# Output projection weights of a hybrid decoder layer: second and third quadrant loaded after the fifth head pair's scores, their differences after the last pair's

## The chip, the cores and the metric

The kernel runs on one core of a Trainium2 chip. The metric is the device time of one execution in microseconds (us); the median of three runs before the change is 560.33 us (558.85 to 560.89). In the profile the engines are called PE (TensorE, matrix products), DVE (VectorE), ACT (ScalarE), POOL (GpSimd) and SP (SyncE, which only issues transfers). Each engine runs its instructions in the order in which the program lists them, so an instruction that waits holds up everything listed behind it on the same engine.

## The reference

One decoder layer on 512 positions of width 1024, in 32-bit floats:

```python
h = rmsnorm(x, norm1_w)
proj = h @ w_in                      # columns for three groups of heads
y_a = dilated_attention(...)         # 6 heads of 64
y_b = gla(...)                       # 4 heads, gated linear attention
y_c = moba_attention(...)            # 6 heads of 64; 512 positions: every past block is taken
mix = concatenate([y_a, y_b, y_c])   # 512 x 1024
x = x + mix @ w_out                  # output projection, w_out 1024 x 1024
h2 = rmsnorm(x, norm2_w)
x = x + square(relu(h2 @ w_ff1)) @ w_ff2
return rmsnorm(x, final_norm_w)
```

The change touches when the weights `w_out` are loaded and when sums of them are made.

## The kernel before

**Precision.** Every large product is made of three: weights and activations are each split into a high part (`wh`, `xh`, `Ah`: a copy by ACT to the reduced float type) and a low part (`wl`, `xl`, `Al`: a subtraction by DVE), and high x high, high x low and low x high are added up in one accumulator bank. `parts` (line 311) does this for a weight block of 128x1024 numbers; it is called by the one stream `cut` (line 333), which takes the blocks one after another, each when one of five pairs of split buffers is free.

**Stages in the order of time.** First a projection for the gated linear attention; then value products (`vps`, in `v_proj`), query and key products of six pairs of heads (`qkps`), the attention of the six pairs; then the second set of value products, the output projection (`ff2(0)`, tiles `f2X`, `f2W`, `f2Y`), and the feed-forward layer. The twelve attention heads are worked as pairs p = 0 to 5, so the "fifth pair" of the title is p = 4 and the last one p = 5.

**Attention of one pair** (`attention`, line 887, one stream for each of the two heads e). A table `nb` of position biases (128x512, 256 KB) is fetched by SP; the one for pair p + 1 is fetched in the middle of pair p. Scores are made on PE for four query blocks in the order 3, 2, 1, 0 into a bank of tag `s` (tile `sps`); there are two such banks. `softmax` (line 994) adds the bias and takes the minimum on DVE (`P<-sps,nb`, which frees the bank) and the exponential on ACT. When the scores of both heads of pair p are listed, the event `("scored", p)` is fired, and for the last pair also the event `"scores"`. The probabilities of pairs 0 to 4 are turned in `moved` (line 1019) and `back` (line 1044): DVE transposes 32x32 blocks (`tb`, `t2s`), SP writes them to DRAM (`turn`), and POOL reads them back in the other order (`thb`, `th`). After the store of both heads the event `("sent", p)` is fired. The last pair is turned by products on PE instead (`ptp`). `values` (line 949) then multiplies probabilities and values, two pairs at a time (tile `po`).

**Output projection.** The 1024x1024 matrix product is done as 2 x 2 quadrants with seven products instead of eight, so sums of quadrants are needed on both sides. The weights' quadrants are called (0,0), (1,1), (0,1), (1,0) in the order of their loading; each is two blocks of 512 KB (`woraw`). `fetch0` (line 444) lists the loads on SP. `sums0` (line 457) makes the sums on DVE:

```python
for ip in range(2):
    t[ip] = b22[ip] - b12[ip]      # product 4, second in order; b22 is (1,1), b12 is (0,1)
for ip in range(2):
    b12[ip] = b12[ip] - b11[ip]    # product 3
```

later `t + b11` for product 2, and `b21 - t` for product 6. `products` (line 494) gives the order of the seven: 0, 4, 6, 2, 3, 1, 5.

**The order of work.** The program is not listed by hand: some thirty streams (Python generators) each yield one operation at a time, and `Plan` (line 112) simulates them while the program is being built. It takes the operation that could start first by its own estimate (at a tie the lower priority number, then the older stream), adds it to its engine's list and moves that engine's clock on. A yield of ("wait", event) or ("take", resource) holds a stream back in this planning. Transfers are modelled as one line of 360 KB per us, longer by a factor for the turned data (line 149); then a time is added until the data count as arrived (line 150): `ZL` for the small transfers of the softmax sums (`zt`), `PL` for POOL's plain transfers, 0.9 us for the others. So any number in the model can change the order of the lists, though no operation is added or lost. On the chip semaphores keep the order correct whatever the estimates; where an estimate is wrong, an engine waits.

All operations are recorded by one helper, so every instruction of the profile has line 142 (L142); they are told apart by the tiles' names.

Of the kernel before, what the change touches and what calls it, by code (L numbers as in the profile page):

```python
# [27 lines left out]
LC, LT, LW, LN, WARM = 1.0, 0.5, 1.0, 0.0, 9  # L28
BIGS, SLOTS, WPAIRS, SCRATCH = 43, 22, 5, 2048
NC = 5  # L30
ZL, PL = 5.0, 3.4
LATE = ((1, 0),)
XP = (0, 1, 2, 3, 4)
NH = 4

# [76 lines left out]
class Plan:  # L112
# [15 lines left out]
    def spawn(self, gen, prio=0):  # L128
        self.streams.append(dict(gen=gen, prio=prio, item=None, at=self.now, sent=None, n=len(self.streams)))

    def fire(self, key, t=None):
        self.done[key] = self.now if t is None else t

    def give(self, res):
        self.free[res].append(self.now)
# [5 lines left out]
    def issue(self, op, at):  # L141
        getattr(getattr(self.nc, op.eng), op.method)(*op.args, **op.kw)  # L142
        t = self.start(op, at)
        if op.eng in self.part:
            self.part[op.eng] = op.part
        self.clock[op.eng] = end = t + op.cost
        if op.method == "dma_start":
            self.clock["dge"] = max(self.clock["dge"], t) + 0.47
            self.clock["dma"] = max(self.clock["dma"], self.clock["dge"] + 0.65) + op.size / 360e3 * (1 + 0.2 * ("turn" in op.outs[0] + op.ins[0]))
            end = self.clock["dma"] + (ZL if op.outs[0][:2] == "zt" else 0.9 if op.eng != "gpsimd" or "accum_op" in op.kw else PL)  # L150
        for n in op.outs:
            self.ready[n] = max(self.ready.get(n, 0.0), end + self.LAT)
        return end
# [57 lines left out]
def hybrid_block_kernel(ctx: ExitStack, tc: tile.TileContext, x0_d, xT_d, x_d, w0_d, wv_d, wqk_d, w1_d, w2_d,  # L211
# [16 lines left out]
    def big(name, dt=F32, shape=(128, 1024)):  # L228
        return wp.tile(list(shape), dt, name=name, tag="big", bufs=BIGS)
# [214 lines left out]
    def fetch0():  # L444
        yield ("wait", ("sent", 3))
        spawn(sums0(), 3)
        for q in ((0, 0), (1, 1), (0, 1), (1, 0)):
            quads[q] = []
            if q in LATE:
                yield ("wait", "vT")  # L450
            for ip in range(2):
                yield ("take", "big")
                quads[q].append(big("woraw"))
                yield SP.dma_start(quads[q][ip], w2_d[0, q[0], q[1], ip])
            fire(("quad", 0, q))

    def sums0():

        yield ("wait", ("quad", 0, (0, 0)))
        t, b6 = [None] * 2, [None] * 2  # L460
        b11 = quads[0, 0]
        B[0] = {0: b11, 4: t, 2: t, 6: b6}
        fire(("B", 0, 0))
        yield ("wait", ("quad", 0, (1, 1)))
        yield ("wait", ("quad", 0, (0, 1)))
        b22, b12 = quads[1, 1], quads[0, 1]
        B[0][5], B[0][3] = b22, b12
        fire(("B", 0, 5))
        for ip in range(2):
            yield ("take", "big")  # L470
            t[ip] = big("t2")
            yield DVE.tensor_tensor(t[ip], b22[ip], b12[ip], op=OP.subtract)
        fire(("B", 0, 4))
        for ip in range(2):
            yield DVE.tensor_tensor(b12[ip], b12[ip], b11[ip], op=OP.subtract)
        fire(("B", 0, 3))
        yield ("wait", ("quad", 0, (1, 0)))
        b21 = B[0][1] = quads[1, 0]
        fire(("B", 0, 1))
        yield ("wait", ("cut2", 0, 4))  # L480
        for ip in range(2):
            yield DVE.tensor_tensor(t[ip], t[ip], b11[ip], op=OP.add)
        fire(("B", 0, 2))
        give("big")
        give("big")
        for ip in range(2):
            yield ("take", "big")
            b6[ip] = big("b6")
            yield DVE.tensor_tensor(b6[ip], b21[ip], t[ip], op=OP.subtract)
        fire(("B", 0, 6))  # L490
# [1291 lines left out]
    spawn(load_fw(), 3)  # L1782
    spawn(load_nw(), 3)
    spawn(fetch0(), 3)
    spawn(fetch1(), 4)
    spawn(fetch2(), 4)
# [95 lines left out]
```

## Time and profile before

| what | us |
|---|---|
| median of three runs | 560.33 |
| these runs, lowest and highest | 558.85, 560.89 |
| the profiled execution | 561.46 |
| its span, first to last instruction | 559.7 |
| PE busy | 547.9 (98%) |
| DVE busy | 488.7 (87%) |
| ACT busy | 350.4 (63%) |
| POOL busy | 84.7 (15%) |

The profile is of one execution. Its page gives for each engine the time in which it worked; busy PE is not PE at its peak, because products overlap and the clock can be lower. The other views used below are: what each engine waited for and for how long in total; the timeline, which lists instructions with start and duration in us from the beginning of the span; windows, which give for a stretch of time the busy time and the number of instructions of each engine, then the granted clock of PE as a share, the share in which the 16 DMA engines were busy and the rate at which they moved data; and the table of transfers with their number, size, and where it is known the median time from issue to landing. An x and a number at the end of a timeline row count instructions of one kind merged into it.

Around the change the order of time is: the scores of the fifth pair between about 153 and 159 us, those of the last pair from 160 to 177, the second set of value products among them up to 184, and the output projection from there to 233.

### The profile page before, as it was taken

The page shows a single profiled execution, that of the slowest core. Times are in us where ns is not written, and L with a number is a line of the kernel's source. Part 1 is how long each engine was busy: PE and PEld are TensorE (multiplying, and loading weights), DVE is VectorE, ACT ScalarE, POOL GpSimd, SP SyncE. Part 2 cuts the span into 40 slices and gives each one's busy share as a digit, 9 for nine tenths or more (in the row PEclk, how much of TensorE's full clock was granted, in tenths as well). Part 3 has the DMA queues.
Part 4 walks back from the last instruction along what each step waited for, and adds up shares of the span by engine and source line. Part 5 has one row for each costly group of instructions (what it writes and reads, how often), then busy time and mean ns, then how long its engine had stood idle before and what let it go on. Part 6 is the DMA issues. An engine that isn't in the chain of part 4 may idle for free.

```text
span 559.7 us, 9429 instructions
## 1 busy us (share of the span) xinstructions
PE 547.9 (98%) x3530; PEld 485.4 (87%) x3530; DVE 488.7 (87%) x793; ACT 350.4 (63%) x588; POOL 84.7 (15%) x135
## 2 busy tenths in 40 slices
PE   9999999999997999999999999999999999999994
PEld 8987888888886888899988899988999888999884
DVE  6969999999976899899999957999679999588985
ACT  7746466756656565669865338864468853479654
POOL 7100000442604000200101100111100111202031
PEclk9999999999998999999999999999999999999999
DMA  8930303799898759902578834669815688937504
GB/s 312 396 127 2 114 3 131 238 271 276 238 298 268 246 184 346 252 5 79 155 178 229 222 117 152 151 168 281 227 39 171 158 237 196 239 70 220 106 0 152
DMA packets 33519, 101.45 MB, mean 181 GB/s; under 512 B 5026, under 2 KB 5712, under 8 KB 33472
## 3 DMA queue, kind: packets, MB, share of 16 engines
q1 hardware_dynamic: 24816, 73.76, 38.7%
q0 software_dynamic: 8368, 26.53, 23.8%
q8 instruction: 28, 0.46, 0.3%
q10 hardware_dynamic: 288, 0.53, 0.3%
q14 instruction: 19, 0.16, 0.1%
HBM read 92.11 MB, written 8.71 MB: 180 GB/s over the span
## 4 chain that ended last, share of the span: by engine, by line
PE 95%; DMA 3%; DVE 1%; issue 1%; ACT 0%; DVEq 0%
PE f2X L142 19%; PE f1V L142 14%; PE qkps L142 12%; PE f2W L142 10%; PE f1W L142 7%; PE vps L142 6%; PE f2Y L142 5%; PE f L142 4%; PE f1X L142 4%; DMA woraw<-in_w 3%; PE po L142 2%; PE sps L142 2%; PE av L142 2%; PE lp L142 1%; PE bk L142 1%; PE bq L142 1%
## 5 line engine op out<-in xcount | busy, mean ns | idle before, releaser
L142 POOL DMA_DIRECT2D w2raw<-in_w x36 | 31.7, 905 | 302.9 <-DVE wl L142 190.3
L142 DVE TENSOR_TENSOR wl<-w2raw,wh 128x1024 fp32r<-128x1024 f32 x56 | 68.4, 1240 | 2.6 <-ACT wh L142 2.6
L142 ACT ACTIVATE wh<-w2raw 128x1024 fp32r<-128x1024 f32 x56 | 58.2, 1050 | 17.7 <-PE f2Y L142 12.5
L142 PE MATMUL f2X<-wh,Ah 128*128 128x512 f32 (+1 forms) x160 | 62.3, 389 | 0.0
L142 PE MATMUL f2X<-wh,Al 128*128 128x512 f32 (+1 forms) x160 | 61.9, 387 | 0.0
L142 PE MATMUL f2X<-wl,Ah 128*128 128x512 f32 (+1 forms) x160 | 61.8, 387 | 0.0
L142 DVE TENSOR_TENSOR wl<-w1raw,wh 128x1024 fp32r<-128x1024 f32 x42 | 50.8, 1222 | 12.3 <-ACT wh L142 12.3
L142 ACT ACTIVATE wh<-w1raw 128x1024 fp32r<-128x1024 f32 x42 | 43.3, 1051 | 29.2 <-DVE w1raw L142 27.6
L142 PE MATMUL f1V<-Uh,wl 128*128 128x256 f32 x168 | 47.5, 283 | 0.0
L142 PE MATMUL f1V<-Uh,wh 128*128 128x256 f32 x168 | 47.5, 283 | 0.0
L142 PE MATMUL f1V<-Ul,wh 128*128 128x256 f32 x168 | 47.5, 283 | 0.0
L142 ACT ACTIVATE h<-h 128x512 f32<-128x512 f32 x53 | 33.3, 629 | 17.8 <-DVE h L142 17.1
L142 ACT ACTIVATE P<-P,mn 128x512 f32<-128x512 f32 (+3 forms) x48 | 26.5, 554 | 20.2 <-DVE mn L142 13.4
L142 PE MATMUL qkps<-xh,wh 128*128 128x512 f32 x96 | 38.2, 398 | 0.0
L142 PE MATMUL qkps<-xh,wl 128*128 128x512 f32 x96 | 37.5, 390 | 0.0
L142 PE MATMUL qkps<-xl,wh 128*128 128x512 f32 x96 | 37.4, 390 | 0.0
L142 PEld LDWEIGHTS f2X<-wh,Ah 128*128 128x128 f32 x160 | 30.1, 188 | 6.9 <-issue 1.0
L142 DVE TENSOR_TENSOR wl<-wraw,wh 128x1024 fp32r<-128x1024 f32 (+1 forms) x32 | 34.6, 1088 | 1.4 <-ACT wh L142 1.3
L142 PEld LDWEIGHTS f2X<-wl,Ah 128*128 128x128 f32 x160 | 30.1, 188 | 6.1
L142 PEld LDWEIGHTS f2X<-wh,Al 128*128 128x128 f32 x160 | 30.1, 188 | 5.8
L142 ACT ACTIVATE Ah<-s 128x512 fp32r<-128x512 f32 x40 | 23.7, 623 | 14.9 <-DVE s L142 14.4
L142 PEld LDWEIGHTS f1V<-Uh,wh 128*128 128x128 f32 x168 | 32.3, 192 | 0.0
(297 smaller groups left out, 1677.3 us busy)
## 6 DMA issues: line engine op xcount, KB each, us to landing
w2raw<-in_w SPq DMA_DIRECT2D x42, 512.0 KB, 5.2
w2raw<-in_w POOLq DMA_DIRECT2D x36, 512.0 KB, 7.4
w1raw<-in_w SPq DMA_DIRECT2D x28, 512.0 KB, 5.3
wraw<-in_wqk SPq DMA_DIRECT2D x12, 512.0 KB, 5.6
turn<-tb SPq DMA_DIRECT2D x10, 512.0 KB, 5.3
thb<-turn POOLq DMA_DIRECT2D x40, 128.0 KB, 5.9
wraw<-in_wv SPq DMA_DIRECT2D x8, 512.0 KB, 8.6
woraw<-in_w SPq DMA_DIRECT2D x8, 512.0 KB, 7.4
```

Of the source, the lines that this page charges most:

```text
L142: getattr(getattr(self.nc, op.eng), op.method)(*op.args, **op.kw)
```

## The change

Three numbers of the planner's model change. The list `LATE` goes. In `fetch0` the loads of quadrant (1,1) wait, in the planning, for the event that the fifth pair's scores are listed; those of (0,1) follow them, and those of (1,0) wait for `vT`, an event of the second value products, as they did before. Quadrant (0,0) is loaded as before, once the fourth pair has been stored. In `sums0` the stream waits for the event `"scores"` before the first subtraction. No operation is added or removed.

```diff
-ZL, PL = 5.0, 3.4
-LATE = ((1, 0),)
+ZL, PL = 4.5, 3.2
...
-            self.clock["dma"] = max(self.clock["dma"], self.clock["dge"] + 0.65) + op.size / 360e3 * (1 + 0.2 * ("turn" in op.outs[0] + op.ins[0]))
+            self.clock["dma"] = max(self.clock["dma"], self.clock["dge"] + 0.65) + op.size / 360e3 * (1 + 0.3 * ("turn" in op.outs[0] + op.ins[0]))
...
         for q in ((0, 0), (1, 1), (0, 1), (1, 0)):
             quads[q] = []
-            if q in LATE:
+            if q == (1, 1):
+                yield ("wait", ("scored", 4))
+            if q == (1, 0):
                 yield ("wait", "vT")
...
         fire(("B", 0, 5))
+        yield ("wait", "scores")
         for ip in range(2):
             yield ("take", "big")
             t[ip] = big("t2")
             yield DVE.tensor_tensor(t[ip], b22[ip], b12[ip], op=OP.subtract)
```

## The prediction

> **What bounds the kernel now.** I read the page first, then what TensorE waited for, then its timeline around the one long wait, then the queues that feed that wait. The page gives the span; the view of TensorE's own waits has three rows (waiting engine, line, releaser: us, times, longest).
>
> ```profile
> span 559.7 us, 9429 instructions
> ```
>
> ```profile
> PE sps L142 <- DVE mn L142: 3.0, 1, 3.0
> PE warm L142 <- DVE eps L142: 1.1, 1, 1.1
> PE vps L142 <- ACT rg L142: 0.6, 1, 0.6
> ```
>
> TensorE is the bound: in 559.7 us it waited 1.1 us at the start, 0.6 us once, and 3.0 us before a score product `sps`; the rest of its idle time is the tail. Only the 3.0 us can be won by order. Its timeline there (start, duration, instruction, in brackets the idle time before):
>
> ```profile
> 167.55 0.39 PE L142 MATMUL vps<-wh,xl 128*128 128x512 f32 x1
> 167.78 0.39 PE L142 MATMUL vps<-wl,xh 128*128 128x512 f32 x1
> 171.13 0.66 PE L142 MATMUL sps<-k,q 128*128 128x384 f32 x1 [2.96 <-DVE mn L142]
> ...
> 172.54 0.63 PE L142 MATMUL vps<-wh,xh 128*128 128x512 f32 x1
> ...
> 174.65 0.39 PE L142 MATMUL vps<-wl,xh 128*128 128x512 f32 x1
> ```
>
> A 512-column product starts 0.23 us after the one before it (167.55 to 167.78). The next should have started at 168.01 and started at 171.13: 3.12 us lost. Then four 384-column products take 1.41 us (171.13 to 172.54) where 4 x 0.23 x 384/512 = 0.69 is normal, and five 512-column ones 2.11 us (to 174.65) where 1.15 is: another 1.68 us, from a slow clock (below). **The stall costs 3.12 + 1.68 = 4.8 us.**
>
> What ended it was VectorE: its queue at the same time,
>
> ```profile
> 164.43 0.13 DVE L142 RECIPROCAL rz<-z 128x4 f32<-128x4 f32 x1
> 167.35 1.22 DVE L142 TENSOR_TENSOR t<-woraw 128x1024 f32<-128x1024 f32 x1 [2.79 <-DMA woraw<-in_w]
> ...
> 169.24 1.23 DVE L142 TENSOR_TENSOR t<-woraw 128x1024 f32<-128x1024 f32 x1 [0.54 <-DMA woraw<-in_w]
> 170.38 0.68 DVE L142 CUSTOM_DVE_ANT_0 P<-sps,nb 128x512 f32<-128x512 f32 x1
> ...
> 171.60 1.22 DVE L142 TENSOR_TENSOR woraw<-woraw 128x1024 f32<-128x1024 f32 x1
> ```
>
> The two subtractions `t<-woraw` (b22 - b12 of the output projection's weights) stand in VectorE's queue ahead of the bias additions `P<-sps,nb` of the last pair, and each waits for its weights to land. The last pair's two first score products occupy both banks of tag `s`; only those additions free them. So TensorE waits for VectorE, and VectorE for a DMA. The issues on SyncE say why that is late (6 weight blocks, then the tables `nb` of the last pair):
>
> ```profile
> 150.59 4.02 SPq L142 DMA_DIRECT2D woraw<-in_w  x6
> 154.71 1.43 SPq L142 DMA_DIRECT2D nb<-tab  x2
> ```
>
> The additions need `nb` too, and the tables are queued behind all six weight blocks. Even without the subtractions ahead of them, the additions could not have run much sooner: two late things lie on top of each other, and the change moves both.
>
> **The change, step by step.** *Four 512 KB loads moved* ((1,1) and (0,1), from before the tables to behind the fifth pair's scores). This brings the last pair's tables forward. How far, I work out from what the DMA engines moved (last columns: granted clock, DMA share, GB/s) and the sizes of the transfers:
>
> ```profile
> 150.60:156.00 5.40, 5.40 (x26) 4.36 (x25) 4.17 (x9) 4.04 (x8) 4.35 (x8) 1.00 0.90 248
> 156.00:162.00 6.00, 6.00 (x32) 5.08 (x31) 5.33 (x19) 5.22 (x15) 0.00 (x0) 1.00 1.04 254
> 162.00:165.00 3.00, 3.00 (x15) 2.49 (x14) 2.56 (x8) 0.72 (x3) 0.00 (x0) 1.00 1.03 326
> 165.00:168.00 3.00, 3.00 (x14) 2.27 (x13) 0.65 (x1) 0.49 (x1) 0.00 (x0) 1.00 1.05 377
> 168.00:171.00 3.00, 0.16 (x1) 0.00 (x0) 2.46 (x6) 0.00 (x0) 0.00 (x0) 1.00 1.02 368
> 171.00:174.00 3.00, 2.87 (x8) 2.44 (x9) 3.00 (x10) 2.14 (x7) 0.80 (x2) 0.53 0.87 281
> ```
>
> ```profile
> thb<-turn POOLq DMA_DIRECT2D x40, 128.0 KB, 5.9
> ...
> nb<-tab SPq DMA_DIRECT2D x8, 256.0 KB
> ...
> turn<-t2s SPq DMA_DIRECT2D x5, 256.0 KB, 7.4
> th<-turn POOLq DMA_DIRECT2D x20, 64.0 KB, 6.8
> ```
>
> Summed from 150.6: 1.34 MB by 156, 2.86 by 162, 3.84 by 165, 4.97 by 168, 6.08 by 171. In the way at 150.6 lie the fourth pair's last turn (0.26 MB) and its read-backs (eight of 128 KB, four of 64 KB: 1.31 MB). With six weight blocks (3.15 MB) this is 4.72 MB, reached at 167.3; the second subtraction started at 169.24, a lag of 1.9 us. Without the last block: 4.19 MB, 165.9, and 167.35 in the trace: 1.4 us. Changed, only two blocks (1.05) stand before the tables (0.26 each): 2.88 MB for the first table, at 162.1, and 3.14 for the second, at 162.8. With lags of 1.4 to 1.9 they are there at **163.5 to 164.0 and 164.2 to 164.7**, against about 170 now. (Estimates; the trace gives the tables no landing of their own.)
>
> *Two subtractions and two more on `woraw` moved behind the last pair's scores* (four of 1.22 us). The additions now wait for the tables alone. At 0.68 us (row 170.38) the first ends near 164.4, the second near 165.1, and the two score products can follow: 6 us before 171.13. Is TensorE there earlier? Its order is written by the planner, which believes in its own DMA times. In the old order thirty value products (6.8 us) fill the time up to 168.0, and the planner was 3.1 us too hopeful over a queue of 18.6 us (150.6 to 169.2). Over the shorter 13.4 us (to 164) the same error is 3.1 x 13.4/18.6 = 2.2 us. The turn factor raised from 0.2 to 0.3 makes the planner slower by 0.1 x 1.57 MB at 0.36 MB/us = 0.4 us: 1.8 left. VectorE's other work (reductions and transposes of the fifth pair up to 164.56, row 164.43) may itself be planned ahead of the additions and then hides all of it. **I take 1.1 us of the wait as left, between 0 and 2.2**, without a clock loss.
>
> The clock: in 171 to 174 the row shows 0.53 after an idle of 2.96 us, and 1.00 up to 168. No row shows a dip after a shorter wait. [...]
>
> *What the moved work does later.* The differences are wanted here:
>
> ```profile
> 182.11 1.23 DVE L142 TENSOR_TENSOR wl<-t,wh 128x1024 fp32r<-128x1024 f32 x1 [0.69 <-ACT wh L142]
> ```
>
> ```profile
> 191.21 4.49 PE po L142 x56
> 195.70 3.67 PE f2X L142 x15
> 199.36 0.68 PE f2W L142 x3
> ```
>
> The loads can be issued once the fifth pair's last score product is out, near 159:
>
> ```profile
> 158.74 0.27 PE L142 MATMUL sps<-klz,q 128*128 128x128 f32 x1
> ```
>
> They follow the tables: 3.14 + 2.10 = 5.24 MB, reached at 168.7, there by 170.1 to 170.6. The subtractions can end by 173, the other two by 175.5. Shifted by the gain, the split `wl<-t` stands at 178.4 and the first product from it (`f2W`) at 195.7. So 3 us and 20 us of cover; the four operations (4.9 us) fall into time in which VectorE now waits for ScalarE. Cost 0; if the cover went, the price would be the lateness itself. The last quadrant (1,0) waits for `vT` as before: 0.
>
> *Queues.* On SyncE the fifth pair's `turn` stores follow the four loads. Bytes ahead of them are the same as now, so their landing hardly moves. GpSimd's read-backs follow the stores:
>
> ```profile
> 173.20 4.35 POOL L142 DMA_DIRECT2D thb<-turn  x8 [18.05 <-PE sps L142]
> 179.23 0.55 POOL L142 DMA_DIRECT2D th<-turn  x1 [1.68 <-DVE rzt L142]
> 180.71 1.63 POOL L142 DMA_DIRECT2D th<-turn  x3 [0.93 <-DMA thb<-turn]
> ```
>
> ```profile
> th<-turn POOLq DMA_DIRECT2D x3, 64.0 KB, 3.5
> ```
>
> The last lands near 181.8 + 3.5 = 185.3. The value products `po` that need it start at 191.21 now, at 187.5 then, and use the last part another 1.8 us later (32 of their 56 products are done first, at 4.49/80 to 4.49/56 each). Cover 4 us: 0.
>
> *Three numbers of the planner* (ZL 5.0 to 4.5, PL 3.4 to 3.2, factor 0.2 to 0.3) change no instruction, only the order from the first turn on. TensorE has no other wait there to win; a new one could cost up to what this one does, 4.8. I take 0, the nearest row being the long stretch without any wait.
>
> **Sum:** -4.8 + 1.1 = -3.7 us. The profiled execution took 561.46 us (559.7 span and 1.8 around it): 557.8. The median of the three runs shown is 560.33, 1.1 less, and the same gain from there gives **556.6 us**.
>
> **Rivals.**
> 1. *The stall stays, for the tables.* If the order puts the last pair's score products as early as 161 to 162 and the tables come at 164.7 or later, TensorE idles 3 us and the slow clock returns: gain 0 to 1.5, so 558.8 to 560.3. For it: all DMA times in this stretch are worse than the planner's. Against: the queue is a third shorter. Chance 0.12.
> 2. *A new wait on the differences.* If the subtractions land in VectorE's queue ahead of the last pair's final additions or reductions, and the weights come at 170.1 to 170.6 while VectorE is there at 168 to 169, the transposes of that pair (`ptp`) come 1.1 to 2.6 us late: 557.7 to 559.2, middle 558.3. For it: the wait is only for the products, not the additions behind them. Against: those additions are ready as the products end. Chance 0.13.
> 3. *Slower: SyncE's queue blocks the fifth pair.* A weight load whose buffer is not yet free waits at SyncE, and behind it wait `turn`, `zt` and `rzb` of the fifth pair. If `turn` lands later by d, the read-backs end at 185.3 + d, against 189.3 for their use. From d = 4 on TensorE waits; from about d = 7 the wait of 3 us brings the clock loss too (4.7) and the gain of 3.7 is gone. At d = 9: 5 + 1.7 - 3.7 = +3.0, so 563.3. For it: four loads now stand just before these stores. Against: the bytes ahead are the same. Chance 0.10 (0.08 of it over the bound). [...]
> 4. *It does not do what it says*: the additions are held by something else and the time stays, 560.3. Chance 0.04: both named causes are in the rows.
>
> **How the numbers follow.** Forecast 0.61, own range 555.3 to 558.0 (rest of the wait 0 to 2.2 gives 555.5 to 557.7, and some scatter). The range that should hold 8 in 10 adds rival 2 and half of rival 1: 555.0 to 559.5. Half a per cent, 2.8 us, is about what a measurement of this kernel tells from no change: faster means under 557.5. From the forecast 0.59 falls there, from rival 2 0.05, from rival 1 0.02: faster 0.66. Slower 0.08, from rival 3. The remaining 0.26 is within.
>
> **What would show it.** In the changed profile: the wait `sps <- mn` is under 2.2 us or gone; the clock stays 1.00 between 160 and 180; the tables are issued before the four weight loads, and the additions of the last pair start between 163.5 and 165 and no `t<-woraw` stands before the last of them; the last `po` starts near 187.5 with no wait. I am wrong if a wait of 3 us stands there again (rival 1), if `ptp` or `po` wait (rivals 2 and 3), or if another stretch that had none shows a wait, which would be the work of the three numbers.

## The result, and the profile after

The changed kernel took **557.38 us** (median of 6 executions, 556.40 to 557.53), against 560.95 us for the kernel before in the same comparison (6, 558.85 to 562.44): ratio 0.9934, interval 0.9913 to 0.9956, so 3.7 us less, between 2.5 and 4.9. A second comparison gave 557.16 us against 560.37: ratio 0.9957, interval 0.9943 to 0.9972, so 1.6 to 3.2 us less. Four executions that took 601 to 1929 us (three of the kernel before, one of a kernel below) are left out of the medians. The profiled execution took 556.40 us. The page of the profile after has the span first, and the shares of the chain that ended last:

```profile
span 554.6 us, 9438 instructions
...
PE 98%; DVE 1%; issue 0%; ACT 0%; DVEq 0%
```

The chain is the work that ended last, followed back from the end of the span. In the kernel before, 3% of it was DMA; now none is. What TensorE waited for in the kernel after (us in total, times, longest):

```profile
PE warm L141 <- DVE eps L141: 1.1, 1, 1.1
PE vps L141 <- ACT rg L141: 0.6, 1, 0.6
```

The row `sps <- mn` is gone altogether. The windows of the kernel after (busy time of PE, PEld, DVE, ACT, POOL, then granted clock, DMA share, GB/s) show a full TensorE and a full clock where 2.84 us of idle time and the clock of 0.53 stood:

```profile
165.00:168.00 3.00, 3.00 (x22) 2.74 (x20) 2.71 (x11) 2.79 (x10) 0.00 (x0) 1.00 1.03 410
168.00:171.00 3.00, 3.00 (x20) 2.53 (x19) 2.71 (x7) 2.47 (x9) 0.00 (x0) 1.00 1.01 402
171.00:174.00 3.00, 3.00 (x20) 2.57 (x18) 2.56 (x5) 1.58 (x3) 2.14 (x4) 1.00 0.33 96
```

SyncE's timeline after the change (the start of an issue, how long issuing took, what, how often):

```profile
145.65 0.33 SPq L141 DMA_DIRECT2D turn<-tb  x1
...
148.85 0.83 SPq L141 DMA_DIRECT2D woraw<-in_w  x2
151.72 0.94 SPq L141 DMA_DIRECT2D nb<-tab  x2
...
153.96 3.90 SPq L141 DMA_DIRECT2D woraw<-in_w  x4
```

Two weight blocks stand ahead of the last pair's tables, four behind. The first row is the second store of the fourth pair, which is ahead of all of this, and it has moved too. In the kernel before it stood here:

```profile
147.41 0.33 SPq L142 DMA_DIRECT2D turn<-tb  x1
```

No yield of the change names it.

VectorE's timeline after:

```profile
162.23 0.65 DVE L141 CUSTOM_DVE_ANT_0 P<-sps,nb 128x512 f32<-128x512 f32 x1
...
164.28 0.68 DVE L141 CUSTOM_DVE_ANT_0 P<-sps,nb 128x512 f32<-128x512 f32 x1
...
168.50 1.23 DVE L141 TENSOR_TENSOR t<-woraw 128x1024 f32<-128x1024 f32 x1 [0.29 <-DMA woraw<-in_w]
169.64 0.28 DVE L141 CUSTOM_DVE_ANT_0 P<-sps,nb 128x128 f32<-128x128 f32 x1
...
169.94 1.20 DVE L141 TENSOR_TENSOR t<-woraw 128x1024 f32<-128x1024 f32 x1
...
176.93 2.35 DVE L141 TENSOR_TENSOR wl<-t,wh 128x1024 fp32r<-128x1024 f32 x2
```

The two large additions, which stood at 170.38 and behind it, now start at 162.23 and 164.28, and neither has a bracket: they waited for no table. One subtraction does stand ahead of the last, smallest addition, and waits 0.29 us for its weights. The score products that need the two freed banks, in TensorE's timeline after:

```profile
163.22 0.33 PE L141 MATMUL sps<-k,q 128*128 128x384 f32 x1
...
165.18 0.34 PE L141 MATMUL sps<-k,q 128*128 128x384 f32 x1
```

The additions end at 162.88 and 164.96 (start plus duration), 0.34 and 0.22 us ahead of these products. So TensorE doesn't wait, but by a small margin.

**Where the time went.** For each profiled execution I took two starts from TensorE's timeline: that of the last `qkps` product (149.78 us in before, 149.76 in after) and that of the first `f2W` product (199.20 and 194.29). Between them lie the same products (about 310 in the traces), in another order, and the stretch is 49.42 us before and 44.53 after. From the first `f2W` to the end of the span it is 360.5 and 360.3 us. So 4.89 of the 5.1 us between the two spans lie in this one stretch. In all kernels below the rest, from the first `f2W` on, is 360.2 to 360.5 us, and I use the stretch to compare profiled executions.

### The profile page after: what moved, and what is told of

Read it like the earlier page. It is cut to its first block, busy times and chain, and to the rows that moved or that the text cites. A ratio compares the mean times of both kernels' runs of the same rounds, so it can differ in the third digit from the quotient of the medians.

```text
span 554.6 us, 9438 instructions
## 1 busy us (share of the span) xinstructions
PE 546.1 (98%) x3530; PEld 484.8 (87%) x3530; DVE 488.0 (88%) x793; ACT 351.2 (63%) x588; POOL 84.6 (15%) x135
## 4 chain that ended last, share of the span: by engine, by line
PE 98%; DVE 1%; issue 0%; ACT 0%; DVEq 0%
PE f2X L141 19%; PE f1V L141 15%; PE qkps L141 12%; PE f2W L141 10%; PE vps L141 8%; PE f1W L141 7%; PE f2Y L141 5%; PE f L141 4%; PE f1X L141 4%; PE sps L141 3%; PE po L141 2%; PE av L141 2%; PE lp L141 1%; PE bk L141 1%; PE bq L141 1%; PE op L141 1%
```

## The experiments

The change has three parts: the loads (the wait for `("scored", 4)`), the sums (the wait for `"scores"`), and the three numbers of the planner's model. First each alone, and all pairs of them but one. (The pair that is missing, loads and sums with the old numbers, lists the same instructions in the same order as the loads alone: with the loads moved, the planner has the subtractions behind the additions already.)

### The loads alone

```diff
+            if q == (1, 1):
+                yield ("wait", ("scored", 4))
             if q in LATE:
```

> Only the four loads are moved behind the fifth pair's scores; the planner's three numbers stay as before, and no wait is put before the subtractions (with the old numbers such a wait changes no engine's list, so this is also both moves without the numbers). Theory (the tables of the last pair were behind six weight blocks, the subtractions ahead of the additions): most of the stall goes, the additions of the last pair start between 163 and 165 us, a rest of 0.5 to 1.5 us may stay because the weights of quadrant (0,0) still start at 150.6: 2.5 to 4.5 us faster than before. Rival (the planner's numbers do it): within 1 us of before. Rival (the subtractions alone block): as the theory, so not told apart here.

Measured: 558.23 us (10 executions), ratio 0.9968, interval 0.9950 to 0.9986. TensorE's wait and two rows of VectorE's timeline in this kernel:

```profile
PE sps L142 <- DVE mn L142: 0.5, 1, 0.5
```

```profile
163.24 0.69 DVE L142 CUSTOM_DVE_ANT_0 P<-sps,nb 128x512 f32<-128x512 f32 x1 [0.80 <-issue]
...
169.52 1.23 DVE L142 TENSOR_TENSOR t<-woraw 128x1024 f32<-128x1024 f32 x1 [0.33 <-DMA woraw<-in_w]
```

The bracket `issue` names nothing that held the addition: the tables were there at 163.24 at the latest, and most of the wait is gone. The subtractions stand behind the large additions although no wait for `"scores"` holds them, so this edit takes both late things away at once. No kernel has the tables early and both subtractions still ahead of the large additions; what the subtractions alone would cost then is not shown. The stretch is 45.70 us.

### The sums alone

```diff
         fire(("B", 0, 5))
+        yield ("wait", "scores")
```

> Only the wait before the subtractions: all four come behind nearly all of the last pair's additions, but the six weight blocks stay ahead of the tables. Theory: the additions still wait for the tables until about 170 us, so a wait of TensorE of 2.5 to 3.5 us and the slow clock behind it stay, and the time is within 1.5 us of before. Rival (the subtractions alone block): the wait goes and it is 3 to 4.8 us faster. It may become slower only if the order after the stall brings a second wait.

Measured: 560.85 us (10), ratio 1.0001, interval 0.9975 to 1.0028: nothing. TensorE's wait, then VectorE's two additions:

```profile
PE sps L142 <- DVE mn L142: 2.0, 2, 1.6
```

```profile
169.04 0.69 DVE L142 CUSTOM_DVE_ANT_0 P<-sps,nb 128x512 f32<-128x512 f32 x1 [3.53 <-DMA nb<-tab]
...
170.05 0.69 DVE L142 CUSTOM_DVE_ANT_0 P<-sps,nb 128x512 f32<-128x512 f32 x1 [0.31 <-DMA nb<-tab]
```

No subtraction stands ahead any more, and the additions wait for the tables themselves, named in the bracket, until 169.04 and 170.05. SyncE began to issue these tables at 154.55, behind six weight blocks; in the changed kernel it began at 151.72, behind two, and they were there by 162.23. Of two late things that lie on top of each other one was taken away, and the other was as late.

### The three numbers alone

```diff
-ZL, PL = 5.0, 3.4
+ZL, PL = 4.5, 3.2
...
-            ... (1 + 0.2 * ("turn" in op.outs[0] + op.ins[0]))
+            ... (1 + 0.3 * ("turn" in op.outs[0] + op.ins[0]))
```

> Only the three numbers of the planner. Theory: six weight blocks and two subtractions still stand ahead, so the stall stays; the fourth pair is stored some 1.7 us earlier, as in the changed kernel (145.65 instead of 147.41 us for its second store), which starts the weights earlier and can shorten the wait by up to that: 0 to 2 us faster than before. Rival (the numbers do it): 3 to 4.8 us faster, no wait left.

Measured: 558.40 us (10), ratio 0.9961, interval 0.9940 to 0.9981. I had put these numbers at nothing; alone they bring about as much as the loads alone. TensorE's wait, SyncE's store of the fourth pair, and VectorE's rows in this kernel:

```profile
PE sps L142 <- DVE mn L142: 0.9, 2, 0.7
```

```profile
145.87 0.33 SPq L142 DMA_DIRECT2D turn<-tb  x1
```

```profile
165.73 1.23 DVE L142 TENSOR_TENSOR t<-woraw 128x1024 f32<-128x1024 f32 x1 [0.97 <-DMA woraw<-in_w]
...
167.00 1.19 DVE L142 TENSOR_TENSOR t<-woraw 128x1024 f32<-128x1024 f32 x1
168.30 0.69 DVE L142 CUSTOM_DVE_ANT_0 P<-sps,nb 128x512 f32<-128x512 f32 x1
```

Both subtractions stand ahead of the additions as in the kernel before, but they are earlier: 165.73 for 167.35, and the first addition 168.30 for 170.38. So is the store, 145.87 for 147.41. (Counted from the last `qkps` product, the first addition is 0.9 to 2.3 us earlier than in the three profiles of before, and the store 1.7.) The last of that pair's transposes shows why, in the kernel before:

```profile
147.11 0.27 DVE L142 STREAM_TRANSPOSE tb<-P 128x128 f32<-128x128 f32 x1
```

and in this one:

```profile
145.58 0.27 DVE L142 STREAM_TRANSPOSE tb<-P 128x128 f32<-128x128 f32 x1
```

The planner lists the fourth pair's transposes earlier on VectorE.

### Loads and numbers, without the sums

```diff
-ZL, PL = 5.0, 3.4
+ZL, PL = 4.5, 3.2
...
-            ... (1 + 0.2 * ("turn" in op.outs[0] + op.ins[0]))
+            ... (1 + 0.3 * ("turn" in op.outs[0] + op.ins[0]))
...
+            if q == (1, 1):
+                yield ("wait", ("scored", 4))
```

> The loads and the numbers, without the wait before the subtractions. The first subtraction then stands ahead of the additions of the last two score products of the first head, not behind the fifth of them. Theory: its weights land at about 168 us, VectorE is there at 167, so it idles about 1 us and the products behind wait 0.3 to 1.3 us: 0.3 to 1.5 us slower than the changed kernel, 2 to 4 us faster than before. Rival (the wait before the subtractions is what counts): most of the gain is lost, within 1 us of before.

Measured: 557.75 us (10), ratio 0.9956, interval 0.9939 to 0.9973. TensorE waits again, and VectorE's timeline says for what:

```profile
PE sps L142 <- DVE mn L142: 0.9, 1, 0.9
```

```profile
169.44 1.22 DVE L142 TENSOR_TENSOR t<-woraw 128x1024 f32<-128x1024 f32 x1 [1.12 <-DMA woraw<-in_w]
170.59 0.28 DVE L142 CUSTOM_DVE_ANT_0 P<-sps,nb 128x128 f32<-128x128 f32 x1
...
170.79 0.42 DVE L142 CUSTOM_DVE_ANT_0 P<-sps,nb 128x256 f32<-128x256 f32 x1
```

Here the first subtraction stands ahead of two additions and waits 1.12 us for its weights, with the additions behind it. This is the mechanism of my second rival, though it holds a score product and not `ptp`, and it costs TensorE 0.9 us. The wait for `"scores"` takes it away; that is what the third part is worth once the other two are made (557.75 to 557.38, which these intervals can't tell from nothing).

### Sums and numbers, without the loads

```diff
-ZL, PL = 5.0, 3.4
+ZL, PL = 4.5, 3.2
...
-            ... (1 + 0.2 * ("turn" in op.outs[0] + op.ins[0]))
+            ... (1 + 0.3 * ("turn" in op.outs[0] + op.ins[0]))
...
         fire(("B", 0, 5))
+        yield ("wait", "scores")
```

> The three numbers and the wait before the subtractions; the loads stay ahead of the tables. Theory: the additions wait for the tables until about 168 to 169 us, as with the numbers alone, and the wait of TensorE stays at 0.5 to 2.5 us; 0 to 2.5 us faster than before, slower than the changed kernel by 1 to 3. Rival (numbers and subtractions together are the cause, the loads add nothing): as fast as the changed kernel.

Measured: 559.49 us (12), ratio 0.9994, interval 0.9978 to 1.0010. TensorE's wait and the first addition:

```profile
PE sps L142 <- DVE mn L142: 2.3, 1, 2.3
```

```profile
168.32 0.69 DVE L142 CUSTOM_DVE_ANT_0 P<-sps,nb 128x512 f32<-128x512 f32 x1 [3.56 <-DMA nb<-tab]
```

Without the loads moved, the tables hold the additions until 168.32, and of the gain of the numbers alone (0.9961) nothing clear of noise is left. The parts don't add up: with the subtractions out of the way the planner lists the score products earlier (the last value product before the wait starts at 166.36 here, at 167.78 in the kernel before), and TensorE reaches the wait sooner.

### All weights behind the fifth pair's scores

The changed kernel, with quadrant (0,0) moved as well:

```diff
-            if q == (1, 1):
+            if q == (0, 0):
                 yield ("wait", ("scored", 4))
```

> As the changed kernel, but the first quadrant (0,0) too is loaded behind the fifth pair's scores, so that the last pair's tables have no weights ahead of them. Theory (what held the additions were the weights ahead of the tables): the tables are there by about 158 to 160 us, no wait is left; as fast as the changed kernel, within 0.5 us, or up to 0.5 us faster if that still waits in some runs. Rival (the weights then come too late for their own use): the split of (0,0) or the subtractions wait, 0.5 to 2 us slower than the changed kernel.

Measured: 557.23 us (5), ratio 0.9955, interval 0.9940 to 0.9970, no wait before `sps`, stretch 44.78 us. The tables are issued at 149.75 us for 151.72, and that buys nothing measurable, since TensorE doesn't wait in the changed kernel either.

### The changed kernel again

No edit; the comparison repeated.

> The changed kernel once more, for a second profile and beside the others on one chip. Theory (no wait of TensorE is left between 60 and 549 us, what differs from run to run is the start): 556.5 to 557.5, again no wait before the last pair's score products, the stretch from the last query and key product to the first f2W near 44.5 us. Rival (the one profile was a lucky run and a rest of about 1 us is usual): a wait of 0.5 to 1.5 us before sps shows, and the stretch is 45 to 46 us.

Measured: 557.16 us (6), with the ratio given above, no wait before `sps`, stretch 44.50 us.

### The kernel before, profiled twice more

My 4.8 us for the stall came from one execution. Two more profiles of the kernel before, without an edit:

> The kernel before, a second profile. The timed runs of before spread over 4 us and the changed kernel's over 1. Theory (the stall hangs on when the DMA lands, and the slow clock comes only behind the longest waits): the stretch from the last query and key product to the first f2W is 46.5 to 49.5 us against 44.5 in the changed kernel, with a wait of 2 to 3.5 us, and without the slow clock if the wait is under about 2.9. Rival (the slow clock is part of every run): 49 to 49.5 us again and a granted clock near 0.5 behind the wait.

> The kernel before, a third profile: as for the second. Of the three profiles of before, at least one without the slow clock by the theory, all with it by the rival.

Measured: 560.34 and 560.75 us. TensorE's wait in the first of them, then in the second:

```profile
PE sps L142 <- DVE mn L142: 1.8, 2, 1.6
```

```profile
PE sps L142 <- DVE mn L142: 2.4, 2, 1.8
```

Both profiles also name the tables in the kernel before itself, which the profile that I had worked from does not. VectorE's second large addition in the later of the two:

```profile
171.46 0.69 DVE L142 CUSTOM_DVE_ANT_0 P<-sps,nb 128x512 f32<-128x512 f32 x1 [0.53 <-DMA nb<-tab]
```

(In the other one it waits 0.19 us for them, until 171.09.) So with both subtractions done the additions still had to wait for the tables: the two late things do lie on top of each other.

In both the granted clock was 1.00 from 162 to 177 us. The stretches are 47.11 and 47.74 us, against 49.42 in the execution that I had worked from and 44.5 in the changed kernel: the stall of these executions is 2.6 and 3.2 us, not 4.9. The mean granted clock of each of the 65 executions of the kernel before in the three later comparisons says how often the slow clock comes: 21 had 0.995 or less, with a median of 562.0 us, and 44 had 0.996 or more, with a median of 559.9. Of 12 executions of the changed kernel, two had 0.995 or less. So about a third of the executions of before have a low clock somewhere and take some two us more, and the profile that I read, at 0.994, was one of them. (Not each of them has it at this place, as the last section shows.)

### The turn factor alone, and PL alone

What the three numbers do was still open. The earlier store was my theory for it; these two kernels change one number each.

```diff
-            ... (1 + 0.2 * ("turn" in op.outs[0] + op.ins[0]))
+            ... (1 + 0.3 * ("turn" in op.outs[0] + op.ins[0]))
```

> Edit: the kernel before with the turn factor 0.3 alone; the two constants, the weight loads and the subtractions as before. The three numbers together made 558.40 us against 560.27. Theory (the three numbers work by the fourth pair's second store: 147.41 us in before, 145.87 with all three, and everything behind it in SyncE's queue comes earlier by as much): the gain goes with the time of that store. In this order two of VectorE's transposes of that pair stand ahead as with all three numbers, but the last one stands behind three multiplications (2.6 us), so the store should come at 147 or later, the tables at 169.5 to 170.5, and the time is 559.8 to 560.5, no gain. Rival (the factor is the number that works, by the order of the pieces around the last pair): 558.2 to 558.8, with the store as late as before. Second rival: the store comes at 146 and the time stays at 560.3: then the store is not what works.

```diff
-ZL, PL = 5.0, 3.4
+ZL, PL = 5.0, 3.2
```

> Edit: the kernel before with PL 3.2 for 3.4 alone. In this order one of the two subtractions stands ahead of the last pair's additions and the other behind the first two, and SyncE issues the six blocks ahead of the tables as before. Theory (the tables come behind six blocks, and when they come goes with the fourth pair's second store): the time goes with that store again; with it near 145.9 the tables are there at 168 to 169 and the time is 558.2 to 558.8; with it near 147.4 they are there at 170 and the time is 560 to 560.5, whatever the subtractions do. Rival (the subtractions ahead of the additions are what holds them): one subtraction less ahead, 1.2 us, so 558.8 to 559.3 with the store as late as in before.

Measured with the factor alone: 561.62 us (12), ratio 1.0010, interval 0.9987 to 1.0033. SyncE's store and TensorE's wait:

```profile
147.61 0.33 SPq L142 DMA_DIRECT2D turn<-tb  x1
```

```profile
PE sps L142 <- DVE mn L142: 2.6, 1, 2.6
```

The store is as late as before, and there is no gain; so far the theory held. (The clock behind this wait was low again, 0.50 from 171 to 174 us.) With PL alone: **564.45 us** (9), ratio 1.0062, interval 1.0041 to 1.0084, slower than before. The same two views, and TensorE's timeline at the longest wait:

```profile
145.67 0.33 SPq L142 DMA_DIRECT2D turn<-tb  x1
```

```profile
PE sps L142 <- DVE mn L142: 3.4, 4, 2.0
```

```profile
165.24 0.39 PE L142 MATMUL vps<-wl,xh 128*128 128x512 f32 x1
167.65 0.44 PE L142 MATMUL sps<-k,q 128*128 128x384 f32 x1 [2.02 <-DVE mn L142]
```

Here the theory failed, and the rival that it was put up against (one subtraction less ahead, 558.8 to 559.3 us) with it. The store is as early as with all three numbers, and VectorE's first large addition starts at 166.90 us, earlier than in any other kernel with six blocks ahead of the tables. But TensorE comes to it at 165.5 instead of 168.0, because this order has the last pair's products earlier among the value products; and it has waits of 0.8 us and less around 152 in the fifth pair's scores, where the kernel before has none. Behind the longest wait the clock is low:

```profile
168.70:172.10 3.40, 3.37 (x9) 2.82 (x10) 3.20 (x6) 1.52 (x4) 1.50 (x3) 0.51 0.55 207
```

The stretch is 51.23 us: of the 6.7 us more than in the changed kernel 3.4 are waits by the view, 1.7 the clock (half of 3.40), and 1.6 I have not divided up. So what a number of the planner is worth is the meeting of two orders, when the tables come and when TensorE arrives, and not the time of one store. In the kernel with all three numbers both are favourable: its store is as early as with PL alone (145.87), and its last value product before the wait starts at 167.98, as late as before (167.78). ZL changes no engine's list, neither alone nor beside the other two, so that kernel is PL and the factor together. Why the planner's order comes out so stays open.

**All together:**

| kernel | median, us | ratio (interval) | wait before `sps`, us | stretch, us |
|---|---|---|---|---|
| before, three profiles | 560.27 (65 executions of the three later comparisons) | | 3.0; 1.8; 2.4 | 49.42; 47.11; 47.74 |
| sums | 560.85 | 1.0001 (0.9975 to 1.0028) | 2.0 | 47.35 |
| sums + numbers | 559.49 | 0.9994 (0.9978 to 1.0010) | 2.3 | 47.26 |
| numbers | 558.40 | 0.9961 (0.9940 to 0.9981) | 0.9 | 46.14 |
| loads (also loads + sums) | 558.23 | 0.9968 (0.9950 to 0.9986) | 0.5 | 45.70 |
| loads + numbers | 557.75 | 0.9956 (0.9939 to 0.9973) | 0.9 | 45.67 |
| loads + sums + numbers | 557.38; 557.16 | 0.9934 (0.9913 to 0.9956); 0.9957 (0.9943 to 0.9972) | none | 44.53; 44.50 |
| the same, all weights | 557.23 | 0.9955 (0.9940 to 0.9970) | none | 44.78 |
| factor | 561.62 | 1.0010 (0.9987 to 1.0033) | 2.6 | 48.72 |
| PL | 564.45 | 1.0062 (1.0041 to 1.0084) | 3.4 | 51.23 |

## Why the prediction was right, and where it was not

The forecast was 556.6 us by 3.7 us less; measured were 557.38 and 557.16 us, inside the range of 555.0 to 559.5 and faster, as forecast; against the bound of 0.5% the first comparison (0.66% faster) lies above it and the second (0.43%) just below. The mechanism held. Two terms of the sum were mis-sized in opposite directions, and that they made up for each other is luck; a third step, the planner's numbers at nothing, was wrong as a matter of mechanism.

**The mechanism.** "Two late things lie on top of each other, and the change moves both" was the centre of it. In the profile that the forecast was made from, the view named the subtractions' weights alone; the two later profiles of that kernel name `nb<-tab` as well, and with the sums moved the additions waited for the tables alone, at a ratio of 1.0001. The estimate for the first table (163.5 to 164.0) was somewhat late: with the loads alone, where the weights are issued when the estimate had them (150.64), the first addition could start at 163.24, and in the changed kernel, where they are issued at 148.85, at 162.23.

**The wait that is left: 1.1 us taken, 0 measured.** On its own profiled execution the sum said 557.8 us, and 556.40 was found. I had the additions end at 164.4 and 165.1, and TensorE 1.1 us ahead of them. They ended at 162.88 and 164.96, and TensorE came to the products that need them at 163.22 and 165.18. The two heads' products, side by side in the kernel before (from 171.13 to 172.54), stand 2 us apart in the new order, so the second addition, hardly earlier than forecast, was early enough.

**"Three numbers of the planner": 0 taken.** This was the step that failed most plainly. With the loads moved the medians differ by 0.9 to 1.1 us (558.23 to 557.38 and 557.16; the intervals of the ratios overlap), and in the profiles the wait left is none against 0.5, the stretch 44.5 against 45.70; by themselves the numbers bring 0.4%, and PL by itself costs 0.6%. I had given the other end as up to 4.8 us on the slow side; PL alone came near it with 3.5 us (0.62% of 560.31). What I left out was the gain: the stretch ahead of the wait shows no wait of TensorE, but it holds the fourth pair's transposes, and the store behind them moved by 1.7 us. The PL kernel has that early store too and is slower, so the store is only one part of it; the other is when TensorE comes to the score products.

**The stall: 4.8 us, carried over to the median.** "The same gain from there" was wrong: 1.68 us of it is the slow clock (0.53 from 171 to 174 us), which only some executions have. The usual stall is 2.6 to 3.2 us by the stretches. 4.8 less 1.1 is 3.7; about 3 less 0, and 1.68 in a third of the executions (a rough 0.6 on average), comes to nearly the same. The 3.7 us of the first comparison therefore don't confirm the sum.

**What the moved work does later: 0, right.** The split `wl<-t` was forecast at 178.4 us and stands at 176.93. The chain that ended last has, in the kernel after, the last value products and the first use of the differences at

```profile
186.30 4.49 PE po L141 x56
190.78 3.67 PE f2X L141 x15
194.45 5.67 PE f2W L141 x25
```

for 187.5 and 195.7 forecast, with no wait. One step of this was wrong all the same: I had the four loads issued near 159, once the fifth pair's last score product is out. They are issued at 153.96. The event is one of the planner's, and fires when it lists that product; what it fixes is a place in SyncE's list, behind the tables, and SyncE gets there when it can.

**Rivals.** *The stall stays, for the tables* is what the sums alone and the sums with the numbers show, but not the changed kernel. *A new wait on the differences* is in the trace: one subtraction stands ahead of the last addition. It found its weights 0.29 us late, where I had put 1.1 to 2.6, and cost TensorE nothing; without the sums' wait one ahead of two additions cost 0.9. So "no `t<-woraw` stands before the last of them" was wrong, and its price smaller than named. *SyncE's queue blocks the fifth pair*: the four loads took 3.90 us to issue and were out at 157.9; the read-backs' timeline on GpSimd shows their start earlier than before (173.20), not later:

```profile
171.86 4.35 POOL L141 DMA_DIRECT2D thb<-turn  x8 [15.12 <-PE ptp L141]
```

## What to carry to other kernels

Where two late things hold the same instruction, taking one away may be worth nothing (1.0001 here) and both about 1.8 us (0.9968, the loads alone), so an experiment with one part alone can say little about the whole. A number in a planner's cost model is an edit of the order, with an unknown cost of either sign (0.4% gained by three numbers, 0.6% lost by one of them): look for whose order ahead of the stall it moves before costing it at nothing. Profile the kernel before more than once before turning a stall into a forecast, since a loss that comes only in some executions (here a granted clock of 0.53) may make up a third of the stall read.

## What the hardware showed that I had not expected

**When the clock falls.** I had tied the slow clock to the longest wait. Start to start, from the last product before the gap to the first one behind it, the gaps of this study were: 3.35 us (before), low clock behind it (0.53 from 171 to 174 us); 2.96 us (the factor alone: 167.92 to 170.88), low (0.50 from 171 to 174); 2.71 us (sums and numbers: 166.36 to 169.07), clock 1.00; 2.41 us (PL alone), low from 168.70 on (0.51), after a second gap of 0.80; 2.21 us (the third profile of before: 168.77 to 170.98), 1.00. So the length of the gap doesn't decide alone: 2.41 us had a low clock behind it and 2.71 had not. And the second profile of before had a low clock without a gap, in windows of the kernel before at the end of the first projection:

```profile
46.00:48.60 2.60, 2.60 (x72) 2.53 (x69) 2.56 (x8) 2.17 (x4) 0.00 (x0) 1.00 0.00 0
48.60:52.30 3.70, 3.43 (x11) 2.35 (x10) 3.70 (x12) 1.81 (x6) 0.00 (x0) 0.54 0.00 0
52.30:54.00 1.70, 1.68 (x7) 1.42 (x8) 0.94 (x4) 1.70 (x3) 0.00 (x0) 1.00 0.03 10
```

What stands ahead of it is TensorE's timeline of that execution:

```profile
45.76 2.01 PE L142 MATMUL lp<-kq 32*128 32x64 f32 x64
47.70 1.05 PE L142 MATMUL dps<-cst,qk 128*128 128x4 f32 x8
48.61 0.65 PE L142 MATMUL vps<-wh,xh 128*128 128x512 f32 x1
```

64 products of 64 columns on 32 rows and eight of 4 columns fill 2.9 us in which the records call TensorE busy (2.60 of the 2.60 us from 46.00), and from 48.60 to 52.30 us the granted clock is 0.54. It did so in this one execution; the other two profiles of before have 1.00 there. Why it fell here is not shown, and neither is what sets the gaps with a low clock behind them (3.35, 2.96 and 2.41 us) apart from those without (2.71 and 2.21 us). By the windows above, the low clock lasts 3.40 us with PL alone (0.51) and 3.70 us here (0.54).

**Scatter that is no edit's doing.** The first value product after the wait for `rg`, long ahead of anything that the change moves, starts at 51.06 us in the first profile of before, at 52.07 in the third and at 52.26 with the loads and the numbers. The span carries such a difference to the end, up to 1.2 us; that is why I compared profiled executions by the stretch and not by the span.
